# A two-layer hybrid transformer in split float32: bias tables moved from the first FFN to the memory's keys, 1/rms one chunk earlier, and two pairs of weight blocks 64 bytes behind a boundary

## The chip, the cores and the metric

One core of one Trainium2 chip runs the whole program in one launch. The metric is the time on the device in microseconds (us), as the median of the runs; the profile is of one further execution. PE is the tensor engine, PEld its weight loads, DVE the vector engine, ACT the scalar engine, POOL the GpSimd engine and SP the queue that issues most transfers.

## What is computed

A sequence of 512 tokens of width 1024 runs through two layers. The first has an FFN, a mixer and an FFN; the second a mixer, a cross-attention over a second memory, an FFN and a last norm.

```python
# layer 1
x = x + 0.5 * swiglu_ffn(rmsnorm(x, ffn1_norm_g), ffn1_w_in, ffn1_w_out)          # f1
o_nsa, o_conv, o_mem = ...   # sparse attention with rel_bias, gated conv, attention over mem
x = x + (g_nsa * o_nsa + g_conv * o_conv + g_mem * o_mem) @ w_out
x = x + 0.5 * swiglu_ffn(rmsnorm(x, ffn2_norm_g), ffn2_w_in, ffn2_w_out)          # f2
# layer 2
x = x + _mixer_block(_rms(x, norm_mix_w), ...)
x = x + _memory_xattn(_rms(x, norm_mem_q_w), _rms(mem_2, norm_mem_kv_w), ...)
x = x + _swiglu(_rms(x, norm_ffn_w), w_ffn_gate, w_ffn_up, w_ffn_down)             # f3
return _rms(x, norm_final_w)
```

`swiglu(h) = (silu(h @ Wa) * (h @ Wb)) @ Wo` with an inner width of 2816, that is 22 units of 128. `rel_bias` is a table of 32 buckets by 16 heads; the sparse attention adds, for each head, a row of it that depends on the distance of query and key.

## The kernel before

**Split products.** Activations lie transposed, 128 features by 512 tokens in each of eight tiles. A float32 product is made of three matmuls (`mm3`): every operand is a high and a low part (`split`: ACT casts the high part, DVE or POOL subtracts for the low one), and low times low is left out. Weights are loaded in blocks of 512 KB by SP into raw tiles (`raw`), split into `wh` and `wl` (`w`), and a chunk of 24 matmuls uses one block.

**FFNs.** `ffn` runs three times (f1, f2, f3). The first three units are `plain`: a chunk for each half, 24 matmuls of 512 columns. `form_x` makes combinations of x's quarters for the other 19 units, and `wforms` those of the weights; `unit` then needs seven products of 256 columns in place of eight (a Strassen scheme): a11, s1, s2, s4, a12, s3 and a22, each a `block` of twelve matmuls. x itself moves in a11, a12 and s4, the combinations t1 to t4 in s1, s2, s3 and a22. Units alternate with the products by `Wo` in three groups, behind units 8, 15 and 22.

**Starts of tiles.** `t` places every tile whose width is a multiple of 64 elements on a 256-byte boundary. The tiles of the combinations (`th`, `tl`) are 64 elements wider and are used from element 48, 192 bytes behind a boundary. `wh` and `wl` start on one.

**1/rms.** The norm's factor is applied behind the products, so x's sum of squares is only needed by then: `rc` (matmuls with ones, then a chain of small DVE instructions) and `rb` (four times two matmuls with the identity, which spread the value over 128 partitions). In `plain`, `rc` is issued behind the first half of the third unit and `rb` behind the second.

**The tables.** `tables` gives a list of steps, which `tick` pops one at a time, in f1 at each finished unit and each product by `Wo`: eight `line` steps (load of `rel` by POOL and of a piece of a one-hot matrix by SP, a matmul, a copy, a store to DRAM by POOL) and eight `rows` steps, each of which writes `dline` for two heads: 128 copies of a line of 640 values, 655 KB, from DRAM to DRAM on POOL's queue. `nsa_scores` loads them as `tab`, `nsa_cmp` those of `dcmp` as `tabc`.

**Memories.** `mem_kv` in the first mixer makes keys (eight chunks of 24 matmuls of 256 columns) and values of the first memory; two of three of its weight blocks have the low part made on POOL. `mem_prep` loads the second memory tile by tile into `mraw`, makes its split and its sum of squares (`macc`).

**Order.** Each engine runs its queue in order. Which instruction comes where in a queue is set by the framework's planner from its own estimates and the order of the text, so instructions of neighbouring steps are interleaved in the trace. `issue_after` (in `behind`) holds a step back until the named matmul in the plan.

## Time and profile before

| | us |
|---|---|
| median of 3 runs | 2512.69 (2512.44 to 2516.0) |
| the profiled execution | 2515.75 |
| its span | 2514.0 |
| PE busy | 2373.9 |
| DVE busy | 1698.5 |
| ACT busy | 1159.3 |
| POOL busy | 442.9 |

The span is the time from the first to the last instruction of the profiled execution; busy time is what an engine spent on instructions in it. Times in the rows below count from the start of the span. A matmul's length in a row contains its way through the array, so that of back-to-back matmuls is read from the distance of their starts. A row of windows gives the stretch, its length, the busy time and (in brackets) number of instructions of PE, PEld, DVE, ACT and POOL, then the mean granted clock, the mean busy share of the 16 DMA engines and GB/s. In a row of waits stand the waiting engine, what it waited for, us in total, number of waits and the longest.

### The profile page before, as it was taken

How to read it: one execution, taken by the hardware profiler on the slowest of the kernel's cores; microseconds unless marked ns; L12 is line 12 of the kernel's file. 1: busy time of each engine (PE TensorE's matmuls, PEld its weight loads, DVE VectorE, ACT ScalarE, POOL GpSimd, SP SyncE). 2: the span in 40 equal slices, each digit the busy share in tenths (PEclk: the TensorE clock that was granted, in tenths of full speed). 3: DMA queues.
4: the chain of work that ended last, by engine and by line, in shares of the span. 5: the costliest groups of instructions: out<-in, count | busy, mean ns of one | idle time of the engine just before them, and what ended most of it. 6: DMA issues, size and time to landing. Idle time of an engine off the chain costs nothing.

```text
span 2514.0 us, 35498 instructions
## 1 busy us (share of the span) xinstructions
PE 2373.9 (94%) x13626; PEld 2054.5 (82%) x13626; DVE 1698.5 (68%) x3149; ACT 1159.3 (46%) x2072; POOL 442.9 (18%) x279
## 2 busy tenths in 40 slices
PE   8974999899999999999999999998999998999997
PEld 6864998797778887887899998787788887789997
DVE  6733778766487757777676776467877367866675
ACT  5412445344355444444553453454665345643453
POOL 1101000242122223222000001212121431000000
PEclk8986999999999999999999999999999999999999
DMA  6525554343122222223445554222222332545551
GB/s 180 171 82 134 160 148 148 98 146 99 56 80 70 75 64 73 74 68 126 126 148 142 157 142 128 74 66 70 67 68 75 115 122 76 136 145 147 157 140 61
DMA packets 100165, 277.45 MB, mean 110 GB/s; under 512 B 18403, under 2 KB 26923, under 8 KB 99868
## 3 DMA queue, kind: packets, MB, share of 16 engines
q1 hardware_dynamic: 82924, 239.81, 29.3%
q0 software_dynamic: 17072, 35.38, 7.4%
q8 instruction: 107, 1.75, 0.3%
q14 instruction: 62, 0.51, 0.1%
HBM read 268.69 MB, written 11.64 MB: 112 GB/s over the span
## 4 chain that ended last, share of the span: by engine, by line
PE 64%; DVE 10%; ACT 3%; issue 2%; DMA 1%; POOL 0%; DVEq 0%; ACTq 0%; POOLq 0%
PE g L231 36%; PE s L231 12%; PE t L231 11%; PE o L231 3%; PE t L239 2%; DVE wl L242 2%; ACT wh L260 1%; DMA wr<-f_s 1%; DVE qk L242 0%; DVE sp L1269 0%; DMA wr<-f_o 0%; DVE cv L254 0%; DVE sm L242 0%; ACT qk L260 0%; DVE o L254 0%
## 5 line engine op out<-in xcount | busy, mean ns | idle before, releaser
L231 PE MATMUL g<-xs,wh 128*128 128x512 f32 (+1 forms) x3022 | 886.4, 375 | 6.9 <-ACT wh L260 4.0
L260 ACT CAST wh<-wr 128x1024 fp32r<-128x1024 f32 (+6 forms) x405 | 409.7, 1015 | 625.3 <-PE g L231 209.1
L231 PEld LDWEIGHTS g<-xs,wh 128*128 128x128 f32 x3022 | 546.7, 191 | 97.7 <-ACT wh L260 7.2
L231 PE MATMUL g<-xs,wl 128*128 128x512 f32 (+1 forms) x1511 | 564.2, 373 | 1.4 <-POOL wl L242 1.2
L242 POOL TENSOR_TENSOR wl<-wr,wh 128x1024 fp32r<-128x1024 f32 (+4 forms) x135 | 313.8, 2325 | 901.3 <-ACT wh L260 671.6
L242 DVE TENSOR_TENSOR wl<-wr,wh 128x1024 fp32r<-128x1024 f32 (+5 forms) x270 | 326.8, 1211 | 81.8 <-ACT wh L260 79.6
L231 PEld LDWEIGHTS g<-xs,wl 128*128 128x128 f32 x1511 | 288.8, 191 | 52.2 <-issue 2.9
L231 PE MATMUL s<-xs,wh 128*128 128x256 f32 (+1 forms) x890 | 225.5, 341 | 8.0 <-ACT xs L260 2.0
L231 PE MATMUL t<-xs,wh 128*128 128x512 f32 (+1 forms) x888 | 224.1, 341 | 0.5 <-ACT e L260 0.4
L561 POOL DMA_DIRECT2D wr<-f_s x57 | 49.4, 872 | 775.8 <-DVE wl L242 174.1
L231 PEld LDWEIGHTS s<-xs,wh 128*128 128x128 f32 x890 | 154.2, 191 | 31.2 <-ACT wh L260 4.2
L231 PEld LDWEIGHTS t<-xs,wh 128*128 128x128 f32 x888 | 153.5, 190 | 20.1 <-ACT e L260 1.2
L231 PE MATMUL t<-xs,wl 128*128 128x512 f32 (+1 forms) x444 | 151.6, 341 | 2.7 <-DVE wl L242 2.7
L231 PE MATMUL s<-xs,wl 128*128 128x256 f32 (+1 forms) x445 | 151.2, 340 | 0.0
L257 ACT ACTIVATE sp<-sp,nm 128x128 f32<-128x128 f32 x192 | 101.9, 532 | 54.3 <-DVE nm L1269 41.5
L242 DVE TENSOR_TENSOR ptl<-t,pth 128x512 fp32r<-128x512 f32 (+1 forms) x128 | 73.4, 603 | 55.5 <-ACT pth L260 55.2
L260 ACT CAST pth<-t 128x512 fp32r<-128x512 f32 (+1 forms) x128 | 62.1, 520 | 92.7 <-PE t L239 92.3
L231 PE MATMUL g<-th,wh 128*128 128x256 f32 x308 | 86.6, 281 | 9.3 <-ACT wh L260 8.8
L231 PEld LDWEIGHTS t<-xs,wl 128*128 128x128 f32 x444 | 84.4, 190 | 13.2 <-DVE wl L242 4.0
L231 PEld LDWEIGHTS s<-xs,wl 128*128 128x128 f32 x445 | 85.0, 191 | 8.8
L231 PE MATMUL g<-th,wl 128*128 128x256 f32 x308 | 86.9, 282 | 1.6 <-DVE wl L242 1.5
L231 PE MATMUL g<-tl,wh 128*128 128x256 f32 x308 | 86.0, 279 | 0.0
(524 smaller groups left out, 4820.3 us busy)
## 6 DMA issues: line engine op xcount, KB each, us to landing
wr<-f_ab SPq DMA_DIRECT2D x73, 512.0 KB, 3.7
wr<-f_s SPq DMA_DIRECT2D x57, 512.0 KB, 3.6
wr<-f_s POOLq DMA_DIRECT2D x57, 512.0 KB, 7.0
wr<-f_o SPq DMA_DIRECT2D x48, 448.0 KB, 3.4
wr<-m_f SPq DMA_DIRECT2D x40, 512.0 KB, 3.6
wr<-m_o SPq DMA_DIRECT2D x40, 512.0 KB, 3.6
w<-f_ab SPq DMA_DIRECT2D x57, 256.0 KB, 4.2
wr<-f_o SPq DMA_DIRECT2D x24, 512.0 KB, 5.1
```

The lines of the kernel that those rows point to most:

```text
L231: self.pm = self.nc.tensor.matmul(o, l, r, start=first, stop=last, skip_group_check=more)
L239: self.nc.tensor.transpose(o, i, self.ident)
L242: (e or self.nc.vector).tensor_tensor(o, x, y, op=op)
L257: return self.nc.scalar.activation(o, x, f, **k)
L260: return self.nc.scalar.copy(o, x)
L561: nc.gpsimd.dma_start(rs, a[key + "_s"][c][:, D:], accum_op=ALU.add)
```

## The change

The steps of `tables` are no longer popped in f1. They become two `line` steps of two matmuls each, with `rel` loaded once and whole one-hot matrices, then one step that stores both results, then the eight `rows` steps; they are popped in `mem_kv`, one behind each key chunk, and the rest behind it. `rc` is issued behind the second unit of `plain` in place of the middle of the third. `wh` and `wl` become 64 elements wider; in `wforms` the pairs a11/a12 and s2/s4 start at element 16 of them, 64 bytes behind a boundary. x's second combination, which moves in s2, is placed at element 0 of `th` and `tl`, and the other three 48 elements further. `mraw` and `vxt` have one buffer in place of two.

```diff
@@ -281,8 +281,7 @@
         self.wi += 1
         raw = self.raw()
         wp, wc, nb = self.wps[self.wi % len(self.wps)]
-        h = self.t(wp, [P, wc], F32R, "wh", nb)
-        l = self.t(wp, [P, wc], F32R, "wl", nb)
+        h, l = (self.t(wp, [P, wc + LINEW], F32R, k, nb)[:, :wc] for k in ("wh", "wl"))
 
         if rows:
             ku, m = rows
@@ -422,18 +421,19 @@
             self.act(xg[-1], self.X[n], AF.Copy, scale=self.cc(self.nk, n))
         x1, x2 = xg
         t = self.t(self.fw, [P, D], F32, "ws", 1)
-        t1, t2, t3, t4 = (t[:, k * H:(k + 1) * H] for k in range(4))
+        t2, t1, t3, t4 = (t[:, k * H:(k + 1) * H] for k in range(4))
         self.tt(t1, x1[:, :H], x1[:, H:], ALU.subtract)
         self.stt(t2, x2[:, H:], -1.0, t1, ALU.mult, ALU.subtract)
         self.tt(t3, x2[:, H:], x1[:, H:], ALU.subtract)
         self.stt(t4, t2, -1.0, x2[:, :H], ALU.mult, ALU.subtract)
 
-        th, tl = (self.t(self.fp, [P, 64 + 4 * H], F32R, k, 4)[:, 48:48 + 4 * H] for k in ("th", "tl"))
-        self.split(th, tl, t)
+        th, tl = (self.t(self.fp, [P, 64 + 4 * H], F32R, k, 4) for k in ("th", "tl"))
+        self.split(th[:, :H], tl[:, :H], t[:, :H])
+        self.split(th[:, H + 48:4 * H + 48], tl[:, H + 48:4 * H + 48], t[:, H:])
         xh, xl = self.xh, self.xl
         lo, hi = slice(0, H), slice(H, S)
         self.B.append([(xh[i][:, lo], xl[i][:, lo]), (xh[i + 4][:, lo], xl[i + 4][:, lo]), (xh[i + 4][:, hi], xl[i + 4][:, hi])]
-                      + [(th[:, k * H:(k + 1) * H], tl[:, k * H:(k + 1) * H]) for k in range(4)])
+                      + [(th[:, k:k + H], tl[:, k:k + H]) for k in (H + 48, 0, 2 * H + 48, 3 * H + 48)])
 
     def end_norm(self):
         self._r = self._rb = None
@@ -508,23 +508,24 @@
         self.bg5 = self.t(g, [P, 16], F32, "bg5", 1)
         self.ts(self.bg5, self.cols[:, o:o + 16], 0.5, ALU.mult)
 
-    def tables(self):
+    def tables(self, p):
 
         nc, a = self.nc, self.a
-
-        def line(key, c, n, dst):
+        box = {}
+
+        def line(key, width, n):
             def go():
-                with self.pool("tab", "right") as p:
-                    rel = self.t(p, [33, 16], F32, "rel", 1)
-                    nc.vector.memset(rel, 1.0)
-                    nc.gpsimd.dma_start(rel[0:32], a["rel"])
-                    oh = self.t(p, [33, n], F32, "oh", 1)
-                    nc.sync.dma_start(oh, a["c_" + key][:, c:c + n])
-                    row = self.t(p, [16, n], F32, "row", 1)
-                    ps = self.ps("o", (16, n))
-                    self.mm(ps, rel, oh, True, True)
-                    nc.vector.tensor_copy(row, ps)
-                    nc.gpsimd.dma_start(dst[:, c:c + n], row)
+                if "rel" not in box:
+                    box["rel"] = self.t(p, [33, 16], F32, "rel", 1)
+                    nc.vector.memset(box["rel"], 1.0)
+                    nc.gpsimd.dma_start(box["rel"][0:32], a["rel"])
+                oh = self.load(key, pool=p)
+                box[key] = self.t(p, [16, 2 * width], F32, key + "l", 1)
+                for j in range(2):
+                    ps = self.ps("t", (16, width))
+                    s = slice(width * j, width * (j + 1))
+                    self.mm(ps, box["rel"], oh[:, s], True, True)
+                    nc.vector.tensor_copy(box[key][:, s], ps)
             return go
 
         def rows(j):
@@ -533,8 +534,11 @@
                 nc.gpsimd.dma_start(self.dline[s], self.drel[s, None, :].to_broadcast([2, P, LINE]))
             return go
 
-        st = [line("oh1", c, LINE // 4, self.drel) for c in range(0, LINE, LINE // 4)]
-        st += [line("oh2", c, 256, self.dcmp) for c in range(0, 1024, 256)]
+        def cmpline():
+            nc.gpsimd.dma_start(self.drel, box["oh1"])
+            nc.gpsimd.dma_start(self.dcmp, box["oh2"])
+
+        st = [line("oh1", LINE // 2, 2), line("oh2", 512, 2), cmpline]
         st += [rows(j) for j in range(8)]
         return st
 
@@ -563,12 +567,11 @@
         r2 = self.t(self.fw, [P, D], F32, "ws", 1)
         out = {}
 
-        def parts(x, k1, k2=None):
+        def parts(x, k1, k2=None, o=0):
             if k2:
                 self.wi += 1
                 wp, wc, nb = self.wps[self.wi % len(self.wps)]
-                h = self.t(wp, [P, wc], F32R, "wh", nb)
-                l = self.t(wp, [P, wc], F32R, "wl", nb)
+                h, l = (self.t(wp, [P, wc + LINEW], F32R, k, nb)[:, o:o + wc] for k in ("wh", "wl"))
             else:
                 h = self.t(self.fw, [P, B], F32R, "h22", 2)
                 l = self.t(self.fw, [P, B], F32R, "l22", 2)
@@ -577,11 +580,12 @@
                 if k:
                     out[k] = h[:, m * B:m * B + B], l[:, m * B:m * B + B]
 
-        parts(ra, "a11", "a12")
+
+        parts(ra, "a11", "a12", 16)
         parts(rs, "s1", "s3")
         self.tt(r2[:, :B], ra[:, :B], rs[:, :B], ALU.add)
         self.tt(r2[:, B:], ra[:, B:], r2[:, :B], ALU.add)
-        parts(r2, "s2", "s4")
+        parts(r2, "s2", "s4", 16)
         parts(r22, "a22")
         return out
 
@@ -653,7 +657,7 @@
         ul.append(l)
         self.tick()
 
-    def plain(self, p, key, c, uh, ul, rms):
+    def plain(self, p, key, c, uh, ul, lag):
 
         pa, pb = self.psf(), self.psf()
         if c == 0:
@@ -665,10 +669,10 @@
                     self.mm3(ps, h[:, s], l[:, s], self.xh[k], self.xl[k], k == 0, k == KT - 1)
         else:
             self.chunk(pa, key + "_ab", 2 * c, self.xh, self.xl)
-            if rms:
-                self.behind(lambda: self.rc)
             self.chunk(pb, key + "_ab", 2 * c + 1, self.xh, self.xl)
-        if rms:
+        if c == lag - 1:
+            self.behind(lambda: self.rc)
+        if c == lag:
             self.behind(lambda: self.rb)
 
         def act():
@@ -717,7 +721,7 @@
 
             wait, lag = [], 2
             for c in range(np_):
-                wait.append(self.plain(p, key, c, *parts[0], c == lag))
+                wait.append(self.plain(p, key, c, *parts[0], lag))
                 if c >= lag:
                     while wait:
                         wait.pop(0)()
@@ -840,7 +844,7 @@
                 if whole:
                     raw = box["raw"][:, m]
                 else:
-                    raw = self.t(p, [P, NMEM], F32, "mraw", 2)
+                    raw = self.t(p, [P, NMEM], F32, "mraw", 1)
                     self.nc.sync.dma_start(raw, self.a[key][:, m])
                 sq = acc if k == 0 else self.t(p, [P, NMEM], F32, "msq", 1)
                 self.act(sq, raw, AF.Square)
@@ -874,6 +878,7 @@
                 self.chunk(ps, "m1_km", c, mh, ml)
                 k = self.t(q, [P, NMEM], F32, "kr", KT)
                 self.mul(k, ps, mrb)
+                self.tick()
                 kr.append(k)
                 s2 = self.t(q, [P, NMEM], F32, "ksq", 5)
                 self.act(s2, k, AF.Square)
@@ -1439,7 +1444,10 @@
                     qr = self.compressed()
                     self.tick(len(self.todo))
                 with self.pool("memkv") as kv:
-                    mem = self.mem_kv(kv)
+                    with self.pool("tab", "right") as tab:
+                        self.todo = self.tables(tab)
+                        mem = self.mem_kv(kv)
+                        self.tick(len(self.todo))
                     es.close()
                     self.mem_heads(*qr, *mem)
             self.rc5 = self.t(g, [P, 4], F32, "rc5", 1)
@@ -1817,7 +1825,7 @@
 
         def xv(vx):
             def evac(i, ps):
-                t = self.t(p, [P, 4, 64], F32, "vxt", 2)
+                t = self.t(p, [P, 4, 64], F32, "vxt", 1)
                 self.ts(t, ps.rearrange("p (a b) -> p a b", a=4), mrc[:, i:i + 1], ALU.mult)
                 v = self.t(p, [P, 4, P], F32R, "vx", 2)
                 self.split(v[:, :, 0:64], v[:, :, 64:128], t)
@@ -1932,7 +1940,6 @@
                 self.norm_sq(j)
             self.end_norm()
 
-            self.todo = self.tables()
             self.ffn("f1", 0.5, self.deferred(step, "mix", True), 3)
             self.upool.__exit__(None, None, None)
             done("d_f1")
```

## Rows read from the trace of the kernel before

**Rows 1.** The page, sections 1 and 2; slices of 62.85 us.

```profile
PE 2373.9 (94%) x13626; PEld 2054.5 (82%) x13626; DVE 1698.5 (68%) x3149; ACT 1159.3 (46%) x2072; POOL 442.9 (18%) x279
...
PE   8974999899999999999999999998999998999997
...
PEclk8986999999999999999999999999999999999999
```

**Rows 2.** Waits of PE, 120 to 252 us: total, times, longest (us).

```profile
PE o L231 <- DMA rel<-rel: 38.0, 3, 17.5
```

**Rows 3.** Timeline of POOL, 90 to 240 us: start and length (us).

```profile
180.07 1.08 POOL L533 DMA_DIRECT2D dline<-drel  x1 [0.24 <-issue]
181.14 0.50 POOL L520 DMA_DIRECT2D rel<-rel  x1
181.63 1.08 POOL L533 DMA_DIRECT2D dline<-drel  x1
```

**Rows 4.** Windows from unit 3 to unit 15 of f1, f2 and f3.

```profile
65.90:294.80 228.90, 174.03 (x1205) 158.96 (x1206) 124.34 (x198) 77.42 (x117) 24.00 (x31) 0.87 0.47 136
1257.20:1419.50 162.30, 161.38 (x1188) 152.47 (x1187) 120.31 (x184) 78.50 (x116) 7.82 (x9) 1.00 0.52 151
2191.60:2358.60 167.00, 162.19 (x1175) 152.73 (x1174) 119.31 (x184) 77.43 (x118) 8.64 (x10) 0.99 0.53 150
```

**Rows 5.** Tile view of rel: ns min/median/max, first to last start.

```profile
L231 PE MATMUL o<-oh,rel x16: 293/416/631, 53.8 to 214.2; 33*16 33x160 f32 x8, 33*16 33x256 f32 x8
```

**Rows 6.** Window over the products of keys and values.

```profile
535.00:585.00 50.00, 50.00 (x320) 45.51 (x319) 31.01 (x47) 23.96 (x33) 26.55 (x11) 1.00 0.56 177
```

**Rows 7.** Waits of PE, 62 to 130 us.

```profile
PE o L231 <- DVE wl L242: 1.7, 1, 1.7
```

**Rows 8.** Windows in f1, five and three dline writes in flight.

```profile
176.00:216.00 40.00, 3.03 (x6) 0.39 (x6) 1.29 (x5) 0.00 (x0) 8.07 (x11) 0.50 0.28 88
182.00:195.00 13.00, 0.00 (x0) 0.00 (x0) 0.00 (x0) 0.00 (x0) 0.71 (x1) 0.50 0.39 131
```

**Rows 9.** Tile view of tab: its loads, first to last start.

```profile
L1256 SPq DMA_DIRECT2D tab<-dline x16: 325/327/454, 659.1 to 1103.4; - x16
```

**Rows 10.** Timeline of f1's start, where 1/rms is made.

```profile
37.00 0.95 PE L231 MATMUL o<-ones,acc 128*128 128x2 f32 x8
...
43.68 0.16 DVE L251 TENSOR_SCALAR rsv<-o 128x8 f32<-128x8 f32 x1
...
48.35 1.23 DVE L242 TENSOR_TENSOR tl<-ws,th 128x1024 fp32r<-128x1024 f32 x1
...
48.60 0.48 PE L231 MATMUL o<-identr,rsh 128*128 128x128 f32 x1 [5.05 <-ACT rsh L260]
```

**Rows 11.** Window with the low granted clock behind it.

```profile
46.00:59.70 13.70, 10.01 (x41) 8.79 (x42) 9.78 (x24) 6.46 (x10) 1.37 (x2) 0.50 0.45 117
```

**Rows 12.** Groups by form: count; busy us, mean ns; idle before.

```profile
L231 PE MATMUL o<-identr,rsh 128*128 128x128 f32 x32 | 9.0, 306 | 9.9 <-ACT rsh L260 9.9
```

**Rows 13.** Timeline of PE in f3: first matmuls of four blocks of twelve.

```profile
2451.06 0.28 PE L231 MATMUL t<-th,h 128*128 128x256 f32 x1
...
2452.42 0.39 PE L231 MATMUL t<-xs,wh 128*128 128x256 f32 x2
...
2453.84 0.40 PE L231 MATMUL s<-xs,wh 128*128 128x256 f32 x2
...
2455.28 0.29 PE L231 MATMUL g<-th,wh 128*128 128x256 f32 x1
```

**Rows 14.** Timeline of SP: the second memory's loads.

```profile
2028.76 1.04 SPq L844 DMA_DIRECT2D mraw<-mem  x2
...
2048.22 0.82 SPq L844 DMA_DIRECT2D mraw<-mem  x2
```

**Rows 15.** Tile view of macc: its use by PE.

```profile
L231 PE MATMUL o<-ones,macc x4: 165/251/251, 2075.4 to 2075.6; 128*128 128x2 f32 x4
```

**Rows 16.** Tile view of dline.

```profile
DMA to landing us min/median/max: 2.5/15.1/21.9
```

## The prediction, made before the changed kernel ran

> **What bounds the kernel now.** I read the page's first two sections, then the stretches in which the tensor engine (PE) is not full, then what it waits for there. PE is busy for 2373.9 of 2514.0 us [rows 1]. So a removed wait counts in full only where PE is idle; elsewhere only fewer or shorter matmuls count. In the 40 slices (62.85 us each) PE has one hole: the fourth slice, 188.6 to 251.4 us, is less than half busy and has the lowest granted clock, 0.6, and the third is at 7 tenths [rows 1]. This is the first FFN (f1), in which the steps of `tables` are popped one by one by `tick`. Between 120 and 252 us PE waits 38.0 us, in three waits, for the load of `rel` [rows 2]. The reason is in the GpSimd (POOL) queue: the load of `rel` at 181.14 was issued right behind a `dline` write [rows 3], and it lands only when that write is through; the longest of the three waits is 17.5 us.
>
> **The tables leave f1.** Price: the same stretch of three FFNs, from the activation of unit 3 to that of unit 15. f1 takes 228.90 us, f2 162.30, f3 167.00; matmuls run are 1205, 1188 and 1175 [rows 4]. f2 and f3 have no tables and PE is 97 to 99% busy in them, so f1 without tables should be like them: 61.9 to 66.6 us less; I take **-64**. This contains the idle time, the table matmuls there, the table writes that delay f1's accumulating loads, and the half-speed work behind the hole.
>
> **The tables arrive beside the keys.** Ticks 1 and 2 of `mem_kv` bring the two lines, tick 3 `cmpline`, ticks 4 to 8 five `dline` writes, and three more follow behind the values; the products of keys and values fill 535 to 585 us. What each queue gets:
> - PE: eight table matmuls with the same 1664 columns as sixteen before; those took 293 ns at least and 416 ns in the median [rows 5]. At 0.2 to 0.4 us for each of the sixteen, 3 to 6 us; those at full clock are the short ones, so **+3**. PE is busy for all 50.00 us of 535 to 585 [rows 6], so nothing hides it.
> - `rel` is loaded once, ahead of all writes, so nothing is queued before it. PE could wait for it once: the nearest rows are 17.5 us behind a write [rows 2] and 1.7 us before a table matmul of f1 with no write ahead of its load [rows 7]. Nearest is the second: **+1**; bounds 0 and 5.
> - POOL: eight writes of 1.08 us and three small ones of 0.50 [rows 3], 10 us in all. Queued behind them are the weight differences (`wl`) of two in three blocks, which PE needs. POOL is busy 26.55 of 50 us there [rows 6], so this fits: 0.
> - DMA: in 176 to 216 us, which held five `dline` writes and little else, the 16 engines were 0.28 busy, 11.2 us of all of them, 2.2 us a write; eight make 18 us [rows 8]. In 535 to 585 the share is 0.56, so 22 us are free [rows 6]. They fit, barely: **+1**; bounds 0 and 18.
> - SP: two one-hot loads, needed only by the table matmuls, between weight blocks that are loaded ahead: 0.
> - Who needs the tables: the first `tab` load is issued at 659.1 [rows 9], 100 us behind the new place: 0.
>
> The share says more: with three writes in flight it is 0.39 of sixteen engines [rows 8], 6.2 of them, so each write sits on about two. The Trainium skill ("DMA: Bandwidth & Descriptors", section "Why a DMA increments its semaphore by 16 and not by 1") says that the slowest dimension of the access pattern limits the engines used; here it is 2. The trace agrees. By that rule a weight block, spread over all engines, would land with the two that also carry a write; the second rival prices it.
>
> **1/rms earlier.** Its matmuls move from the middle of the third chunk pair to the end of the second, one chunk of 24 matmuls earlier. In f1 they ended at 37.95 and the chunk at 43.55 (48.60 less the 5.05 idle); VectorE (DVE) took them up at 43.68, between the work that forms x's combinations; PE got `rsh` at 48.60 and had idled 5.05 us [rows 10]. From 46.0 to 59.7 the granted clock was 0.50, the 1.2 GHz level, with PE busy 10.01 us [rows 11]; at 2.4 GHz half of it, 5 us, falls away if PE does not idle. Together 10 us. Against it: the last combination's low half starts at 48.35 and takes 1.23, to 49.58 [rows 10], and unit 3 needs it. Between 43.68 and 48.35 DVE also runs the chain's dozen small instructions, like the first (0.16 us, 0.2 with the gap behind it); without them it would end near 47.2, and s2's weights, sums that DVE makes behind it, near 50. PE, free at 43.55, reaches that block near 48 and waits some 2 us. So **-8**; bounds 0 (the chain stays as late on DVE's queue) and -11. Before all `rsh` casts of the kernel (eight row casts) PE idles 9.9 us [rows 12], of which f1 has 5.05; f2 and f3 are two of the other seven, and I give them 0.
>
> **The 64 bytes.** Of the seven products of a unit, three have x itself as moving operand (a11, a12, s4) and four a combination, stored 192 bytes behind a 256-byte boundary. All weights start on a boundary. Twelve matmuls of a combination take 1.36 us (2451.06 to 2452.42), 113.3 ns each; twelve with x take 1.42 (to 2453.84) and 1.44 us (to 2455.28), 118.3 and 120.0 [rows 13]. The difference is 5.0 and 6.7 ns; I take 5, as some combinations are slower than this one. After the change a11, a12 and s4 have x on the boundary and weights 64 bytes behind one: the distance of the two, modulo 256, is that of the four fast ones. s2 and x's second combination change places at the same distance. If the distance decides, 3 blocks x 12 matmuls x 19 units x 3 FFNs = 2052 matmuls gain 5 ns: **-10**; bounds from -14 (6.7 ns) to +4, if the moving operand's own offset decides: then x stays slow and s2's 684 matmuls lose 6 ns. I take the distance, since two streams are read at once and one pair of offsets alone is seen slow. PE is the bound in those stretches [rows 4], so the gain is not hidden.
>
> The Trainium skill speaks against this part: by "TensorE: Matmul & The Clock Gate", section "Step-by-step: what each phase is for", the engine has two independent read ports, and loading the next weights takes no read bandwidth from the running matmul. By that rule this term is 0. 113.3 and 120.0 ns for one shape [rows 13] do not fit a rule without addresses, but no row has shifted weights.
>
> **The small rest.** `form_x` makes two splits of one: one more ACT and one more DVE instruction, twelve times, of which f1's four are near the path: **+0.5**. The second memory's raw tile has one buffer in place of two: loads come in pairs, the first at 2028.76, the fourth at 2048.22, 6.5 us apart; one by one, seven such intervals end them at 2074 at the latest, beside a first use at 2075.4 [rows 14, 15]. Behind a load that waits on SP stand `m2_mo` and `x2_k` blocks, which are loaded ahead. **+1**; bounds 0 and 6. `vxt` with one buffer delays one evacuation by a split, and wider weight tiles keep every other start on a 256-byte boundary: 0.
>
> **Sum.** -64 +3 +1 +1 -8 -10 +0.5 +1 = -75.5. The profiled execution took 2515.75 us (span 2514.0), so 2440 on its terms; the median of the runs shown is 2512.69, 3 us lower, so I predict **2437**.
>
> **Rivals.**
> 1. Weight offsets do nothing (the rule of the two ports; this part then doesn't do what it says): the -10 is missing, 2447, or 2451 with s2's loss. For: no row shows shifted weights. Against: two times for one shape, which differ in nothing else that is shown.
> 2. The `dline` writes hold up the weights of `mem_kv`: all 18 us of DMA time land on PE, 2437 - 1 + 18 = 2454. For: two engines of sixteen carry each write, and a key block is needed every 2.9 us (24 matmuls of 0.12). Against: three buffers ahead, a mean share of 0.56.
> 3. The start does not come back, since weights and combinations are late there anyway: 2445.
> 4. Slower than before: POOL cannot issue a `dline` write until the one before has landed. Landing takes 15.1 us in the median [rows 16]; seven such waits are 106 us, with the weight differences queued behind, so PE stands: 2437 + 106 = 2543. It decides from the sixth full wait (6 x 15.1 = 91 us against 75.5 of gain). Against: at 181.63 a write was issued in 1.08 us, 1.56 us behind the one before, which was in flight [rows 3].
>
> **How the numbers follow.** Forecast 0.58, rival 1 0.18, rival 2 0.11, rival 3 0.08, rival 4 0.02; 0.03 for the rest (above all another order of the queues, which the planner makes anew). Around the forecast, -64 has 2.6 to either side, the start 3, the 64 bytes 4, the tables' place 4: some 12 us if most fall to one side, 2425 to 2449; rivals 1 to 3 reach from 2445 to 2454, and two of them at once to 2464. Range **2425 to 2460**. About 0.2%, 5 us, is what a measurement of this kernel can tell from no change; only rival 4 and part of the rest are not faster by that: faster 0.96, same 0.02, slower 0.02.
>
> **What would show it.** Right: f1's stretch from unit 3 to 15 near 160 us; no clock of 0.5 from 170 to 235 us, nor at unit 3; twelve x matmuls in 1.36 to 1.38 us; `dline` writes between 540 and 600 us with PE full there. Wrong: x blocks still at 1.42 us (rival 1); waits on `wl`, `wh` or `rel` of over 5 us beside the keys (rivals 2 and 4); a wait for `rsh` at unit 3 (rival 3).

## The result, and the profile after

The changed kernel takes 2475.1 us (median of 4 runs, 2472.9 to 2476.1) beside 2512.6 for the kernel before: 0.985 of it (95% interval 0.983 to 0.988), 37.5 us less. The forecast was 75.5 less, so the sign is right and half of the size is missing. The page of the changed kernel, sections 1 and 2, answers to [rows 1]:

```profile
PE 2373.4 (96%) x13618; PEld 2055.2 (83%) x13618; DVE 1691.0 (68%) x3150; ACT 1160.3 (47%) x2084; POOL 435.1 (18%) x266
...
PE   8999998969999999999999999998999998999997
...
PEclk9999999789999999999999999899999998999998
```

The hole of the fourth slice is gone, and a smaller one has come: in the eighth and ninth (slices of 61.85 us, so 433 to 557 us) the granted clock is at 7 and 8 tenths, and in the ninth PE is busy for 6 tenths. These are the keys and values of the first memory, where the tables went. PE's busy time has hardly moved, 2373.9 to 2373.4 us: part of what is counted there runs at half clock. Windows of the changed kernel, f1 and f2 from unit 3 to unit 15, answer to [rows 4] (f3: 161.70 us):

```profile
62.90:223.90 161.00, 159.84 (x1171) 150.73 (x1170) 117.87 (x181) 76.09 (x115) 8.60 (x10) 1.00 0.55 156
1222.90:1385.50 162.60, 161.67 (x1188) 152.61 (x1187) 120.30 (x184) 78.44 (x117) 7.80 (x9) 1.00 0.53 150
```

f1 is now like the others: 228.90 became 161.00. What it gave was partly lost at once. Two stretches tell it. The first runs from f1's last store of x to the first product of the memory's scores (`s<-kmh`): the kernel before,

```profile
436.80:598.80 162.00, 153.16 (x834) 129.69 (x833) 110.83 (x198) 63.57 (x92) 61.42 (x27) 0.98 0.40 125
```

and the changed one, with two parts of it below:

```profile
367.30:557.30 190.00, 161.60 (x784) 133.25 (x783) 110.05 (x203) 61.20 (x90) 66.75 (x36) 0.85 0.40 125
460.70:488.10 27.40, 27.40 (x108) 21.69 (x108) 13.62 (x33) 6.42 (x11) 7.86 (x6) 0.50 0.32 87
511.90:532.40 20.50, 10.68 (x29) 7.64 (x30) 12.14 (x31) 5.46 (x12) 3.35 (x2) 0.50 0.22 80
```

28 us more, with fewer matmuls. The two parts alone, 48 us, ran at the 1.2 GHz level; the mean granted clock of 0.85 makes it some 56 of the 190 us. The DMA share is the same 0.40 in both. The second stretch is the whole mixer, to the first reload of x: 729.3 us before, 765.9 after. So the balance of the profiled spans is: f1 with its start 436.8 to 367.3 (-69.5), mixer 1 +36.6, the rest 1347.9 to 1340.9 (-7.0), in all 2514.0 to 2474.1.

What PE waits for in 460 to 557 us of the changed kernel (nothing in [rows 6] answers to it; PE was full there):

```profile
PE t L231 <- DVE ksq L242: 7.3, 1, 7.3
PE g L231 <- ACT wh L260: 3.5, 3, 2.3
PE g L231 <- POOL wl L242: 2.8, 1, 2.8
PE t L239 <- DVE mr2y L254: 2.5, 1, 2.5
```

Behind `ksq` stand the Squares on ACT, and ACT waits there for weights (total, times, longest):

```profile
ACT wh L260 <- DMA wr<-m_vm: 18.0, 4, 8.4
```

The issues of the changed kernel (bytes, median us to landing): a write took 15.9 us to land in the kernel before and the values' weights 4.7 (the trace has the landing of only two of the eight `m_vm` blocks, before and after; ACT's waits say more).

```profile
dline<-drel POOLq DMA_DIRECT2D x8, 640.0 KB, 18.4
wr<-m_vm SPq DMA_DIRECT2D x8, 512.0 KB, 6.5
```

And POOL's queue, which answers to [rows 3]:

```profile
482.89 1.11 POOL L534 DMA_DIRECT2D dline<-drel  x1
...
491.83 1.09 POOL L534 DMA_DIRECT2D dline<-drel  x1
501.59 1.05 POOL L534 DMA_DIRECT2D dline<-drel  x1 [8.67 <-PE g L231]
502.66 2.35 POOL L242 TENSOR_TENSOR wl<-wr,wh 128x1024 fp32r<-128x1024 f32 x1
```

The fourth write stood 8.67 us on POOL although the matmul that the row names was long done; it went out 18.7 us behind the first, which is a write's landing time, and the weight difference behind it is the 2.8 us wait above.

Three explanations offer themselves. **O**: the planner now puts the chain of the key norms (`ksq`, `mr2y`, `hr`) ahead of most values, in the kernel before behind them, and its latency lies bare. **T**: the table matmuls keep the clock low. **W**: the writes hold up the weights, because each sits on two of sixteen engines (W2) or on POOL's queue (W1).

### The profile page after: what moved, and what is told of

Same layout as the page of the kernel before. It is cut to its first block, busy times and chain, and to the rows that moved or that the text cites. A ratio compares the mean times of both kernels' runs of the same rounds, so it can differ in the third digit from the quotient of the medians.

```text
span 2474.1 us, 35466 instructions
## 1 busy us (share of the span) xinstructions
PE 2373.4 (96%) x13618; PEld 2055.2 (83%) x13618; DVE 1691.0 (68%) x3150; ACT 1160.3 (47%) x2084; POOL 435.1 (18%) x266
## 4 chain that ended last, share of the span: by engine, by line
PE 64%; DVE 11%; ACT 3%; issue 3%; DMA 1%; POOL 1%; DVEq 0%; ACTq 0%; POOLq 0%
PE g L231 36%; PE s L231 12%; PE t L231 11%; PE o L231 3%; PE t L239 2%; DVE wl L242 2%; ACT wh L260 1%; DVE qk L242 1%; DMA wr<-f_s 0%; POOL wl L242 0%; DVE sp L1274 0%; DVE cv L254 0%; DMA wr<-m_gm 0%; DMA wr<-f_o 0%; DMA wr<-m_vm 0%
## 5 line engine op out<-in xcount | busy, mean ns | idle before, releaser
L231 PE MATMUL g<-xs,wh 128*128 128x512 f32 (+1 forms) x3022 | 875.9, 372 | 10.3 <-ACT wh L260 6.0
```

Source lines behind the costliest of these rows:

```text
L231: self.pm = self.nc.tensor.matmul(o, l, r, start=first, stop=last, skip_group_check=more)
```

## Experiments beside the keys

**The chain behind the values again**, with a hold on the last product of the values:

```diff
-            self.head_rows(r, self.mem_rms(q, sq, 2), 4, 2)
+            self.behind(lambda: self.head_rows(r, self.mem_rms(q, sq, 2), 4, 2))
```

> The changed kernel with one edit: the chain that makes the key norms of the memory (sums of squares ksq, transposes of mr2y, products with hr) is held back until the last product of the values, where the kernel before has it; tables, writes and weights stay in place. Theory O (the planner put this chain ahead of most values, where nothing covers its 7.33 + 2.47 + some 3 us of waiting, and the low clock of 20 us at 511.9 follows from that idle time): mixer 1 from 848 to about 828, total 2455. Theory W (the writes hold POOL and the weights; the chain's place is only where the loss shows): the wait for the values' weights takes its place, total 2470 to 2475. Theory T (the table matmuls themselves): 2475.

Measured: 2481.1 us (2480.0 to 2483.8). The stretch is 190.0 us again, to the tenth. O falls; PE waits in it for

```profile
PE g L231 <- POOL wl L242: 6.8, 2, 6.6
PE g L231 <- ACT wh L260: 5.7, 3, 4.0
PE g L231 <- DVE wl L242: 4.9, 1, 4.9
```

and ACT 31.6 us for the landing of `m_vm` blocks. With the chain out of the way the late weights stop PE directly.

**The writes later**: the eight `rows` steps popped behind `mem_heads` in place of `mem_kv`.

> The changed kernel with one edit: the eight dline writes are issued behind mem_heads, not beside the keys and values; the table matmuls stay, and the norm chain stands where the changed kernel has it. Theory W (writes hold POOL and the weights, so that the Squares of the keys on ACT come late): wl's 2.8 us and most of ksq's 7.3 us and the low clock behind them go, mixer 1 from 848 to about 828, total 2455. Theory O (the chain's place costs, whatever the weights do): 2470, waits of ksq, mr2y and hr stay at over 10 us together. Theory T (the table matmuls keep the clock low): the 27 us of 0.5 at 460 stay in any case, some 12 us of the loss.

Measured: 2468.2 us (2460.0 to 2469.4); the stretch 179.1. The edit did a part of what was meant: the text's place doesn't hold a transfer back, and the plan issued six of the eight between 482 and 552 us all the same. It speaks for W, no more.

**The lines ahead of f1**, the `rows` steps left in `mem_kv`:

```diff
-                    with self.pool("tab", "right") as tab:
-                        self.todo = self.tables(tab)
-                        mem = self.mem_kv(kv)
...
+                    self.todo = self.late
+                    mem = self.mem_kv(kv)
...
+            with self.pool("tab", "right") as tab:
+                st = self.tables(tab)
+                for go in st[:3]:
+                    go()
+                self.late = st[3:]
             self.ffn("f1", 0.5, self.deferred(step, "mix", True), 3)
```

> The changed kernel with the two lines (their loads, four table matmuls, copies and stores) made ahead of the first FFN, the writes still beside the keys; the plan then puts the norm chain behind the values by itself. Theory T (the table matmuls, eight instructions of 0.7 to 1.1 us behind matmuls of 4 columns, keep the clock at 0.5 for 27 us): no low clock at 460 to 488 but the 3.4 us of the kernel before; with the chain's place mended too, mixer 1 near 815 to 820, the start 3 to 6 us longer: 2448. Theory W: the writes stay, so wl's wait and late value weights stay, 2460. Theory O: as with the chain held back, less the table matmuls' 5 us: 2452.

Measured: 2486.1 us (2484.1 to 2501.3). The plan drew the writes forward here: they are issued from 24 to 245 us, all in f1. The mixer's stretch is 161.7 us, that of the kernel before, and f1 ends at 417.2 in place of 367.3. So eight writes with no table matmul near them cost f1 some 43 us (49.9 less 7 for the lines at the start, as the next run shows). PE has no long wait there, but many (60 to 380 us, the largest):

```profile
PE g L231 <- ACT wh L260: 9.1, 6, 4.4
PE s L231 <- ACT wh L260: 6.0, 7, 1.3
```

and the clock of 50 to 367 us is 0.93. This is what the run above could not show: W, and in f1 as well. At most two writes were in flight at once here and none stood on POOL, so the cost doesn't need a write that stands.

**The same, with each write held behind a weight difference of the keys on POOL** (`issue_after`), so that the writes stand where the changed kernel has them and only the table matmuls, copies and stores are missing.

> The changed kernel with the two lines made ahead of the first FFN, as in the run before, and now each dline write held behind a weight difference of the keys on POOL, so that the eight writes stand where the changed kernel has them and none in f1. In the mixer the writes are there, the table matmuls, their copies and the two small stores are not. From f1's last x to the first product of the memory's scores (190.0 us in the changed kernel, 162.0 in the kernel before, 161.7 with neither): Theory W (the writes cost): 182 to 190, total 2472 to 2480 with 3 us more at the start. Theory T (the table matmuls cost): 162 to 168, total 2452 to 2458, f1 without a wait of weights.

Measured: 2478.4 us (2473.2 to 2481.3); the stretch is 180.1:

```profile
374.30:554.40 180.10, 149.70 (x777) 127.44 (x776) 107.56 (x198) 61.21 (x90) 65.67 (x33) 0.90 0.42 128
```

So of the 28 us the table matmuls and what goes with them are 10 and the writes 18 (over the whole mixer, 765.9 to 761.4 us, the first part is only 4.5). At the start they cost 7 of these 10 us (f1 ends at 374.3, not 367.3).

**Sixteen engines for a write.** One transfer for each head, whose outermost dimension is the 128 copies and not the two heads, at the same places of POOL's queue:

```diff
-                nc.gpsimd.dma_start(self.dline[s], self.drel[s, None, :].to_broadcast([2, P, LINE]))
+                for h in range(2 * j, 2 * j + 2):
+                    with self.tc.issue_after(self.lp.ins):
+                        nc.gpsimd.dma_start(self.dline[h], self.drel[h, None, :].to_broadcast([P, LINE]))
```

> The changed kernel with each head's line written by a transfer of its own whose outermost dimension is the 128 copies, so that it is spread over all sixteen engines and not two; POOL issues sixteen in place of eight, at the same places; table matmuls in place. Theory W2 (a write takes two of sixteen engines, and a weight block, which needs all of them, lands with these two): landing of a write from 18 us to below 6, weights of keys and values landing in 3 to 4 us, the 190.0 us stretch 165 to 175, total 2450 to 2460. Theory W1 (POOL's own time and queue cost, not the engines): POOL gets 8 us more, 192 to 200, total 2478 to 2485. Theory T: 190, 2475.

Measured: 2452.7 us (2447.5 to 2459.2), 0.975 of the kernel before (0.973 to 0.977). The stretch,

```profile
367.90:541.20 173.30, 159.65 (x841) 131.97 (x840) 116.50 (x203) 63.65 (x92) 71.17 (x46) 0.96 0.46 149
```

the issue of the writes,

```profile
dline<-drel POOLq DMA_DIRECT2D x16, 320.0 KB, 7.6
```

and all that is left of PE's waits from 460 to 541 us:

```profile
PE t L239 <- DVE mr2y L256: 2.5, 1, 2.5
PE t L231 <- DVE vct L242: 0.8, 1, 0.8
PE g L231 <- POOL wl L242: 0.8, 1, 0.8
```

Same bytes, and the mixer is 29.3 us shorter (736.6 in place of 765.9). The plan here puts the norm chain behind the values, so the nearer neighbour is the run that only did that: between the two, 771.9 to 736.6 us, the form of the writes differs and the hold on POOL that goes with it here. PE's waits for weights went from 17.4 us to 0.8, ACT's for `m_vm` from 31.6 to 12.0. POOL issues sixteen transfers and not eight, so the time that POOL takes to issue them falls as the main cause. What this run doesn't separate is how much came by the weights' own landing and how much by a write that stands on POOL ahead of a weight difference: with spread writes none stands. The Trainium skill ("DMA: Bandwidth & Descriptors", section "Why a DMA increments its semaphore by 16 and not by 1") has the engines chosen by the slowest dimension of the access pattern: 2 in the one form, 16 in the other. The trace agrees: three writes in flight kept 0.39 of sixteen engines busy in [rows 8], up to six of the new ones, together with the weights, 0.98:

```profile
486.00:498.00 12.00, 11.23 (x90) 10.76 (x90) 5.05 (x6) 3.89 (x6) 7.91 (x9) 1.00 0.98 341
```

**Both**, issued by POOL or by SP:

> Both edits: lines ahead of the first FFN, writes spread over sixteen engines and issued by POOL beside the keys. If writes and table matmuls each cost part: the 190.0 us stretch near 163 to 166, total 2450. If POOL's issuing costs: 170 to 180, total 2460 to 2468.

> The same with the sixteen writes issued by SP between the weight blocks of the keys and values, so that POOL has none of them. If POOL's queue is what costs, 162 to 164 in the stretch and 2447; if the bytes cost, wherever they are issued, as the run with POOL; if SP's loads come late behind sixteen more transfers, waits of PE on wh of the values, 170 to 180.

Measured: 2446.2 (2443.3 to 2449.1; 0.972 of before, 0.971 to 0.974) and 2445.8 us (0.971, 0.969 to 0.973), the best versions found, 29 us ahead of the changed kernel. The stretch is 165.8 and 172.5, the whole mixer 727.8 and 735.5; POOL's part in issuing is worth nothing that shows in the total. The run on POOL and the run before the spread writes (2478.4 us) differ in the text by the form of the writes alone, with the same hold in both: the stretch goes from 180.1 to 165.8 us and the mixer from 761.4 to 727.8, 33.7 us.

**The kernel before with spread writes**, tables left in f1:

> The kernel before with one edit: each head's line is written by a transfer of its own whose outermost dimension is the 128 copies, so over sixteen engines; tables stay in f1, everything else as before. Theory W2 (two engines of sixteen): the loads of rel behind a write land in 2 to 6 us in place of 14 to 20, the three waits of 38.0 us shrink below 12, f1's stretch from unit 3 to 15 from 228.9 to 180 to 195, total 2465 to 2480. Theory Q (rel's place behind writes in POOL's queue, however they land, as the forecast had it): the bytes before rel are the same, waits of 25 us or more stay, total above 2495.

Measured: 2467.0 us (2461.3 to 2472.5), 0.982 of before (0.980 to 0.984): more than the whole change brought (46 us and 37.5, though the two intervals just meet), by one edit and with no step moved in the text. The plan moved some: all sixteen writes go out between 89 and 114 us, where the eight of the kernel before went out from 87 to 200. f1 from unit 3 to 15, 228.90 us in [rows 4]:

```profile
67.20:249.90 182.70, 170.96 (x1205) 158.02 (x1206) 123.93 (x198) 78.18 (x117) 23.67 (x39) 0.96 0.60 170
```

and PE's largest waits from 50 to 260 us, with 38.0 us for `rel` in [rows 2]:

```profile
PE o L231 <- issue: 8.9, 2, 7.4
...
PE o L231 <- DMA rel<-rel: 2.0, 1, 2.0
```

The longer of the two waits that the profile puts down to nothing ("issue") is for `rel` too: it was issued at 101.53, behind writes and a load of weights, landed 8.3 us later at 109.8, and PE took it up at once:

```profile
109.88 0.58 PE L231 MATMUL o<-oh,rel 33*16 33x256 f32 x1 [7.43 <-issue]
```

So the two largest waits for `rel` are 9.4 us together, in place of 38.0 in three. Directly behind a write `rel` lands in both kernels some 0.2 us after it: 14.9 us after its issue behind the write of 180.07 in the kernel before, whose landing took 15.8, and 3.3 us after its issue at 89.63 here, right behind a spread write, which landed after 3.6. Its place in the queue counts, and what it costs is the landing time of what stands ahead.

**The tables alone**, offsets and 1/rms as before (single buffers and wider weight tiles stay):

> The changed kernel with 1/rms and the offsets both as before, so the kernel before with the tables (and the single buffers of mraw and vxt) moved alone. From the runs with one part undone each (2479 and 2482, the changed kernel 2475): 2482 to 2486, of which f1 gives some 66 less and the mixer 37 more than the kernel before.

Measured: 2485.1 us (2482.9 to 2489.8): 28 of the 37.5 us.

## Experiments on the offsets and on 1/rms

**Offsets undone**, and **1/rms in the third unit again**:

> The changed kernel with the 64-byte offsets alone undone: weights a11/a12 and s2/s4 start on a boundary again, x's combinations stand all at element 48 as before. Theory A (from the changed kernel's trace: x blocks went from 118.3-120.0 to 117.5-117.8 ns a matmul, s2 from 113.3 to 117.5, so nothing is left over): 2475, within 3 us either way, and twelve x matmuls take 1.42 to 1.44 us again, twelve of s2 1.36. Theory B (the prediction's: the offsets gained 10 us, hidden in the total by other losses): 2485.

> The changed kernel with the matmuls of 1/rms in the middle of the third unit again. Theory A (the start gained 3 us by them, as unit 3's activation came at 62.9 in place of 65.9, and f3 5 us): 2478 to 2483, with rsh 4 to 5 us late again at f1's unit 3 and a clock of 0.5 over some 14 us there. Theory B (the place does nothing outside the start): 2478. Theory C (the start's 3 us come from the tables leaving f1's first ticks, not from 1/rms): 2475.

Measured: 2479.0 us (2470.5 to 2484.1) and 2481.9 (2481.0 to 2482.2). The first can't be told from the changed kernel. Why shows in the starts of f3's blocks, s2, a22, s4, a12 and the next, in the changed kernel, which answers to [rows 13]:

```profile
2408.89 0.28 PE L231 MATMUL g<-th,wh 128*128 128x256 f32 x1
2410.30 0.29 PE L231 MATMUL t<-th,h 128*128 128x256 f32 x1
2411.69 0.40 PE L231 MATMUL t<-xs,wh 128*128 128x256 f32 x2
2413.10 0.40 PE L231 MATMUL s<-xs,wh 128*128 128x256 f32 x2
2414.51 0.29 PE L231 MATMUL g<-th,wh 128*128 128x256 f32 x1
```

x's blocks take 1.41 us (117.5 ns a matmul) in place of 1.42 and 1.44, but s2, at 113.3 in the kernel before, takes 1.41 as well, and a22 behind it 1.39 (115.8). In the median of the steady units (25 and 27) the seven blocks sum to 9.76 us before and 9.77 after.

The second removes the wait for `rsh` and gets another. In the changed kernel PE's one wait from 40 to 70 us is

```profile
PE s L231 <- DVE z L242: 4.5, 1, 4.5
```

and with 1/rms back it is that for `rsh`, 5.1 us, once more. DVE's timeline of the changed kernel tells why:

```profile
45.99 0.69 DVE L242 TENSOR_TENSOR ws<-wr,wr 128x512 f32<-128x512 f32 x1
...
48.57 1.23 DVE L242 TENSOR_TENSOR wl<-ws,wh 128x1024 fp32r<-128x1024 f32 x1 [1.17 <-ACT wh L260]
...
50.44 0.68 DVE L242 TENSOR_TENSOR z<-s,rb 128x512 f32<-128x512 f32 x1
```

The spread 1/rms is there at 45, but the weight sums of unit 3 stand ahead of `z` on DVE, and `z` has to empty the bank that PE's next product writes. f1 ends 2.3 us later with 1/rms back, and 2.5 us earlier with it back where the offsets are back too (369.0 and 371.5): no gain at f1's end. Yet both pairs differ by 6 to 7 us in the total, 2.5 and 6.0 us of it in the profiled mixers, which the edit doesn't touch. Some of this may be scatter: in the two runs below with zeros behind the end, where the text up to there is that of the changed kernel, the mixer took 769.5 and 771.2 us in place of 765.9. The rest stays open. Unit 3 scatters too: it comes at 62.3 to 64.9 us in six traces whose text up to there is that of the changed kernel (62.9), at 68.3 with the offsets undone, and at 65.6 to 67.2 in four with the late 1/rms.

**A block of zeros** behind the last output, 24 matmuls for each pair of starts (moving operand, weights, in elements), and **x at element 48** in all tiles, then **at element 32** (these two also take the wider weight tiles back):

> The changed kernel with a block of matmuls of zeros behind the last output: 24 matmuls of 256 columns for each of sixteen pairs of starts (moving operand at element 0, 16, 32, 48 of a 256-byte line, weights at 0, 16, 32, 48), then 24 of 512 columns for four pairs. Theory A (the moving operand's own start decides): 113.3 ns for every pair with the moving operand at 48, 117 to 120 at 0, whatever the weights' start. Theory B (the distance modulo 256 decides): 113.3 on the diagonal moving minus weights = 48 elements, 120 elsewhere. Theory C (neither: what writes into the same memory meanwhile decides): all pairs within 1 ns of each other. For 512 columns: 227 ns at all (B, C) or some 7 to 13 less at moving 48 (A). The block itself adds some 70 us.

> As the one with the offsets undone, and x's two parts stand at element 48 of their line in all eight tiles, so that x moves 192 bytes behind a boundary in a11, a12, s4 and in all 512-column products. Theory A (the moving operand's own start decides): three x blocks of a unit go to 113.3-115 ns, 3 x 12 x 57 x 5 ns = 10 us less than with the offsets undone, and if the 512-column matmuls gain 6 ns as well, some 5000 of them another 30: 2435 to 2465. Theory B (distance or something else): 2475.

> As x at element 48, but x's two parts at element 32 of their line, 128 bytes behind a boundary, all weights on one. In the block of zeros, matmuls of 512 columns took 228.7 ns at distance 0, 233.3 at 16 or 48 elements and 222.3 at 32; with x at 48 those of the kernel went from 227 to 231 to 232. Theory D (the distance decides, each width in its own way): 512-column matmuls with x near 221 to 222, 4600 of them x 5 = 23 us less than with the offsets undone (2479), x blocks of 256 columns 118.6 in place of 118.3 to 120: 2455. Theory E (the block of zeros is not like the kernel): 2475 to 2490.

In the block of zeros 256 columns took 119.7 ns at distance 0 (three pairs; the fourth ran at half clock), 117.7 to 118.1 at 16 or 48 and 118.6 at 32, worked out from the starts of each 24; 113.3 was not seen. So the distance does count, by 1.6% and not by 6%. 512 columns took 228.7 at (0, 0), 233.3 at (48, 0) and (0, 16), and 232.2 at (48, 16): the last 24 matmuls start at

```profile
2528.12 0.39 PE L231 MATMUL g<-mvh,sth 128*128 128x512 f32 x1
...
2533.46 0.40 PE L231 MATMUL g<-mvh,stl 128*128 128x512 f32 x1
```

That is 23 distances in 5.34 us, none under 228 ns. The 222.3 that the expectations for x at 32 and for the second block below name is what comes out, nearly, if 24 are counted; no run shows it, so there was no reason to expect 2455 of x at 32. x at 48 gave 2490.4 us (2487.9 to 2498.4), x at 32 2489.5 (2485.6 to 2492.2), both some 11 us slower than with the offsets undone. With x at 48 two rhythms of the same blocks stand close together (first matmuls of x blocks):

```profile
2385.94 0.40 PE L231 MATMUL s<-xs,wh 128*128 128x256 f32 x2
2387.36 0.40 PE L231 MATMUL t<-xs,wh 128*128 128x256 f32 x2
...
2396.15 0.39 PE L231 MATMUL s<-xs,wh 128*128 128x256 f32 x2
2397.51 0.39 PE L231 MATMUL t<-xs,wh 128*128 128x256 f32 x2
```

1.42 us a block at 2386 and 1.36 at 2396, with the same starts. Over the whole kernel the fast rhythm prevails: the seven blocks of a unit sum to 9.52 us in the median. So theory A's 113.3 ns came for x's blocks, though the distance is that of the changed kernel, where they take 117.5. But the 512-column products of the mixers went from 227 ns to 232 or 233 (mixer 1 takes 764.1 us with the offsets undone, 772.9 with x at 48), and that outweighs it. x at 32 gave 232 there too (771.7 us), as the zeros at a distance of 32 had.

**A second block of zeros**, with the pairs in another order:

> The changed kernel with a second block of zeros at its end, 24 matmuls for each pair (moving start, weight start): 256 columns at (0,0), (48,0), (0,16), (48,0), (0,0), (48,0), (32,0), (48,0), (16,0), (48,0), (48,0), then 512 columns at (0,0), (48,0), (0,0), (48,16), (0,0), (32,0), (32,0). Theory H (what ran before decides): (48,0) behind (0,0) 113.3 ns, behind (0,16) or another pair 117.7; 512 columns at (48,16) behind (0,0) 232, not the 222.3 of the first block. Theory S (the pair alone decides): (48,0) 117.7 everywhere, as in the first block, and (48,16) 222.3.

First matmuls of the 24 at (0,0), (48,0), (32,0), (48,0), (16,0), (48,0), (48,0), and the one behind:

```profile
2483.88 0.28 PE L231 MATMUL t<-mvh,sth 128*128 128x256 f32 x1
2486.74 0.29 PE L231 MATMUL g<-mvh,sth 128*128 128x256 f32 x1
2489.48 0.28 PE L231 MATMUL s<-mvh,sth 128*128 128x256 f32 x1
2492.32 0.28 PE L231 MATMUL g<-mvh,sth 128*128 128x256 f32 x1
2495.15 0.28 PE L231 MATMUL t<-mvh,sth 128*128 128x256 f32 x1
2497.98 0.28 PE L231 MATMUL g<-mvh,sth 128*128 128x256 f32 x1
2500.71 0.28 PE L231 MATMUL s<-mvh,sth 128*128 128x256 f32 x1
2503.43 0.39 PE L231 MATMUL t<-mvh,sth 128*128 128x512 f32 x1
```

(48, 0) takes 2.74 us behind (0, 0), 2.83 behind (32, 0), 2.73 behind (16, 0) and 2.72 behind itself: 113.3 to 114.2 or 117.9 ns for one pair. So the pair alone doesn't decide. What ran before fits better, as H has it, though not by H's list: behind (16, 0), and earlier in the block behind (0, 16), the fast rhythm came too. Which tile the products go to changes from pair to pair as well and wasn't held fixed. 512 columns at (48, 16), behind (0, 0), took 232 here as in the first block, and 233 at (32, 0).

**The best version with x at 48 in the FFNs alone**:

> Lines ahead of the first FFN and spread writes on POOL beside the keys (2446), with the weights' offsets undone and x's parts at element 48 in the three FFNs alone, at 0 in the mixers. If x at 48 gives 0.23 us a unit as in the run with it everywhere (9.53 in place of 9.76) and nothing is lost elsewhere: 57 units, 13 us less, 2433. If half the units stay in the slower rhythm, as f3's did there: 2438 to 2442. If the units' gain goes into waits: 2446.

Measured: 2448.0 us (2442.4 to 2448.4) beside 2446.2 without it: nothing in the total, although the units did get faster (9.52 us in the median in place of 9.77). f1 ends 4.8 us earlier, the mixer takes 7.7 more and the rest 1.8 more; what takes the gain back behind f1 stays open.

## Why the prediction was right or wrong

| step | predicted | measured |
|---|---|---|
| tables leave f1 | -64 | -67.9 (228.90 to 161.00) |
| tables beside the keys: matmuls +3, `rel` +1, DMA +1, POOL 0 | +5 | +36.6 |
| 1/rms earlier | -8 | unit 3 comes 3.0 earlier in this trace; nothing at f1's end |
| 64 bytes | -10 | 0 |
| small rest | +1.5 | none to be seen |
| not in the sum: behind mixer 1 | 0 | -7 |

**Tables leave f1: right, for half of the reason.** The comparison with f2 and f3 held without knowing the cause. The cause named, `rel`'s place in POOL's queue behind a write, was half of it: `rel` does land with the write ahead, but that this takes 14 to 20 us is the writes' form. With spread writes, still in f1, f1 ends at 392.3 in place of 436.8, 44.5 of the 69.5 us (some of it perhaps by the other order of the plan). The slow writes were the load on f1, by `rel` and, as the run with the lines ahead of f1 shows, by the weights.

**Beside the keys: the step that failed is "they fit, barely: +1".** It added up mean shares of sixteen engines, 18 us of work and 22 us free. The same part of the forecast had read from [rows 8] that a write sits on two engines, and the rule of the Trainium skill that it cites said the same; the forecast then priced it as the second rival at 0.11, "against: three buffers ahead, a mean share of 0.56". The writes were in flight from 483 to 566 us, the weights landed late, and PE stood or ran at half clock (10.68 us busy of 20.50 at 511.9): 29 to 34 us by the two pairs of runs with and without spread writes. The rival's mechanism was right, and its 18 us too small: it counted DMA time alone, and the low clock came on top (0.85 in the stretch, 0.98 before); how much of it is the clock wasn't separated. The table matmuls were mis-sized too: +3, measured 7.5 to 10 with their copies and stores (the stretch without them: 190.0 to 180.1, and 173.3 to 165.8 with spread writes; the whole mixer 4.5 and 8.9). POOL's "0" missed that a write can stand on the queue, the fourth rival in small: not one write at a time but three.

**1/rms:** the working named the chain behind it (weight sums on DVE, "waits some 2 us") and under-sized it: 4.5 us, for `z`. The clock from 46.0 to 59.7 us rose from 0.50 [rows 11] to 0.88, but the time came back as waiting.

**64 bytes:** the step "the distance decides" failed, and its bound "to +4" was near. The distance is worth some 2 ns in the zeros, 0.8 to 2.5 for x's blocks in the kernel, not 5 to 6.7, and s2 lost 4.2 at an unchanged distance.

**The 7 us behind mixer 1** stay with either part undone (1342.1 and 1341.3 us from mixer 1's end, before 1347.9), and 4.3 of them with both undone; which buffer or order brings them wasn't tried. That they and the tables' gain in f1 were larger than forecast hid part of the loss beside the keys; this was luck.

Of the signs named beforehand, f1 near 160 us and the waits on `wl` and `wh` beside the keys (6.3 us together) both came, and the second was the sign of rivals 2 and 4. x's blocks at 1.41 us are nearer to rival 1's 1.42 than to the 1.36 to 1.38 hoped for.

## What to carry to other kernels

Before moving a slow transfer out of the way of something, ask why it is slow: eight broadcast writes with an outermost dimension of two cost 43 us in one place and 29 in the other, and rewriting them over sixteen engines (46 us) brought more than moving them (28). A mean DMA share hides this; compare one transfer's share and landing time with those of its neighbours. And where a wait disappears in a chain that several engines feed, look at what is next on the same queue: it was 4.5 us where 5.1 had been.

## What was not expected of the hardware

- Two-head writes (256 copies of 2560 bytes) were in flight three at a time at most, and a fourth that was due stood on POOL until a landing (8.67 us in the changed kernel). Of one-head writes six were in flight at once, the same 768 copies, and none stood; whether six is their limit wasn't tried.
- Matmuls of one shape and one pair of starts run in one of two steady rhythms, 113.3 or 117.7 ns for 256 columns, and the starts alone don't decide which; in the zeros it changed with what ran before. For 512 columns 227 to 233 ns were seen in the zeros, 227, 232 and 233 in the kernels.
- PE can be granted 0.50 while the profile shows it busy all the time: 27.40 of 27.40 us from 460.7, behind 26 matmuls of 4 columns and with the table matmuls (33 rows by 16 columns) in it. The table matmuls alone don't do it: with them in the same place the clock was at 0.50 for 6.8 us in the run with the chain behind the values, and for 3.4 and 6.8 us in the one with spread writes. What else it takes stays open.
